# Wider joint projections of two linear attentions, with the gates projected between them

## The chip, the cores and the metric

The kernel runs on one core of a Trainium2 chip. The metric is the device time of one execution in microseconds (us); lower is better.

The engines are named as in the profile: PE multiplies matrices (PEld loads its stationary operand), DVE works on vectors, ACT applies functions and copies, POOL is GpSimd, SP issues most of the transfers. DMA engines move the data.

## The reference

A decoder trunk of two layers over 512 tokens of width 1024. Every layer has a half-step feed-forward block, a mixer and a second feed-forward block. The mixer projects the normalised tokens h once and gives the columns to three groups of heads; the outputs are joined and projected back:

```python
proj = h @ w_in
(g_q, g_k, g_v, g_g, g_lr, n_q, n_kc, n_vc, n_ks, n_vs, n_kw, n_vw, n_gate,
 r_q, r_k, r_v, r_g) = split(proj)
o_gla = rms_norm(gla_chunked(g_q, g_k, g_v, log_a)) * silu(g_g)
o_nsa = nsa_attention(n_q, ...)
o_ret = group_norm(retention_chunked(rotary(r_q), rotary(r_k), r_v)) * silu(r_g)
out = concat([o_gla, o_nsa, o_ret]) @ w_out
```

The first and the third are linear attentions of 4 heads each (256 columns for each of q, k, v and gate). The second is a sparse attention of 8 heads: it adds a compressed, a selected and a windowed softmax attention.

## The kernel before

Every large product is made three times on PE in reduced fp32 form: weights and activations are split into a high part and a low rest (whi, wlo and hh, hl), and high x high, high x low and low x high are summed (mm3, L439 to L445). The weights come as chunks of 128x1024 numbers in an order that plan and plan_mixer write down once (class Weights): a DMA on SP's queue (L164), an ACT copy that makes whi (L176), and a subtraction that makes wlo on DVE, or on POOL for the names in ON_POOL (L177). Chunks are split two ahead of their use; there are three buffers for raw chunks and four for split ones.

The framework has a scheduler of its own: on each engine it may start a later instruction whose inputs are ready while an earlier one waits, and it prefers what is emitted first. So the order in the source is a priority and no fixed sequence. At run time each engine follows the sequence that the scheduler chose.

The mixer of a layer (mixer, L737) emits, in this order:

1. A common unit x (L788 to L790), then the projection vc, with the tokens as the moving operand (proj_t, 24 matmuls of 128x512).
2. The value projection gv of the first linear attention by proj_n (L710): here the tokens are the stationary operand and 256 weight columns move (L721 to L723). It makes 96 matmuls and uses two PSUM banks. Its result is copied to gv by ACT (L817).
3. The compression network of the sparse attention (compress, L901).
4. For each of two head pairs: projections gq and gk, then gla_pair (L932 to L994).
5. Value projection rv (L838), then for each of two pairs: rq, rk with rotary, and ret_pair (L1027 to L1060). rotary (L727) lets ACT make raw (or qraw), SP exchange halves into sw by four DMAs, POOL multiply by the sine (L733) and DVE do the rest (L734, L735).
6. Projections ks, kw and nq0 to nq3 with rotary (krot, qrot, qraw).
7. The temporary pool is closed; the pools of oh, ol, nh, nl and of the sparse attention are opened in its place. nsa (L1084) emits cmp (the compressed softmax, L1123 to L1145), stack_k and stack_q (kh, kl, qk: L1101 to L1113), then gates: proj_n for gg and rg, Silu into sg on ACT (L869), a multiplication by the norm's weights on POOL (L872).
8. lin_out (L1064): the linear outputs onat times their statistics (L1073) and times sg (L1075), transposed on PE (L1078) into oh (ACT, L1080) and ol (DVE, L1081).
9. The weave: score of one unit (query block qc, kind) beside apply of the unit before it. score makes the products (L1162, L1165 to L1167), the maximum on DVE (L1169), the exponentials on ACT (L1172) and the normalisation (L1174 on); apply transposes (L1197), copies (L1200, L1202) and multiplies by the values (L1207). The last apply of a query block ends in nh (L1213).
10. The output projection: the half of the linear attentions, from oh and ol, in the single bank "f" (8 x 12 matmuls, by L443 to L445, and a DVE addition L451), then the half of the sparse attention.

Of eight PSUM banks, three ("mm") and one ("f") rotate through bank(); three "t" serve transposes and small products, and one is "o". The weight chunks of a layer's mixer come in the order x, vc, gv, gq0, gk0, gq1, gk1, rv, rq0, rk0, rq1, rk1, ks, kw, nq0 to nq3, gg, rg, wol, won.

Of the kernel before, what the change touches and what calls it, by code (L numbers as in the profile page):

```python
# [7 lines left out]
F32 = mybir.dt.float32  # L8
# [3 lines left out]
AF = mybir.ActivationFunctionType  # L12
# [12 lines left out]
ON_POOL = ("gg", "gq0", "kw", "rv")  # L25
# [10 lines left out]
def _cols(name, start, n):  # L36
# [11 lines left out]
       for i in range(4)]  # L48
)
N_UNITS = [("gv", _cols("g_v", 0, 256)), ("gg", _cols("g_g", 0, 256)),  # L50
           ("rg", _cols("r_g", 0, 256)), ("rv", _cols("r_v", 0, 256))]
# [161 lines left out]
class Build:  # L213
# [273 lines left out]
    def plan_mixer(self, l):  # L487
        W, a = self.W, self.a

        def n_unit(i):  # L490
            for s in range(2):
                self.u[l, "n", N_UNITS[i][0], s] = W.add(a["wn"][l, i, :, 1024 * s:1024 * s + 1024], D, N_UNITS[i][0] in ON_POOL)

        def t_unit(*names):
            for n in names:
                i = [x[0] for x in T_UNITS].index(n)
                self.u[l, "t", n] = W.add(a["wt"][l, i], D, n in ON_POOL)

        for i in range(KC // 2):
            self.u[l, "x", i] = W.add(a["wx"][l, :, 2 * NXK * i:2 * NXK * (i + 1)], 2 * NXK, i == 2)  # L500
        t_unit("vc")
        n_unit(0)
        t_unit("gq0", "gk0", "gq1", "gk1")
        n_unit(3)
        t_unit("rq0", "rk0", "rq1", "rk1")
        t_unit("ks", "kw", "nq0", "nq1", "nq2", "nq3")
        n_unit(1)
        n_unit(2)
        for key in ("wol", "won"):
            for q in range(KC // 2):  # L510
                self.u[l, key, q] = W.add(a[key][l, q], D)
# [198 lines left out]
    def proj_n(self, l, name):  # L710
        nc = self.nc
        ps = [self.bank((128, 2, 256)) for _ in range(2)]
        for s in range(2):
            wh, wl = self.use(l, "n", name, s)
            for k4 in range(4):
                k = 4 * s + k4
                cs = slice(256 * k4, 256 * k4 + 256)
                for c in range(4):
                    ts = slice(128 * c, 128 * c + 128)
                    o = ps[c // 2][:, c % 2, :]  # L720
                    nc.tensor.matmul(o, self.hh[:, k, ts], wh[:, cs], start=(k == 0 and c % 2 == 0), stop=False)  # L721
                    nc.tensor.matmul(o, self.hh[:, k, ts], wl[:, cs], start=False, stop=False)  # L722
                    nc.tensor.matmul(o, self.hl[:, k, ts], wh[:, cs], start=False,  # L723
                                     stop=(k == KC - 1 and c % 2 == 1))
# [12 lines left out]
    def mixer(self, l):  # L737
# [11 lines left out]
        with tc.tile_pool(name="mtmp", bufs=1, reuse_waits="tile") as tp:  # L749
# [65 lines left out]
            ps = self.proj_n(l, "gv")  # L815
            for i in range(2):
                nc.scalar.activation(gv[:, 2 * i:2 * i + 2, :], ps[i], AF.Copy)  # L817
# [6 lines left out]
            for pr in range(2):  # L824
# [7 lines left out]
                drain(self.gla_pair(l, pr, e, q, k, gv, a2, lrT, onat, stats))  # L832
            self.cos, self.sin = ld("cos", [128, T]), ld("sin", [128, T])
            self.dm, self.gq = ld("dm", [128, 4, 128]), ld("gq", [128, 2, 128])
            rv = tp.tile([128, 4, 256], F32, name="rv", tag="w1", bufs=2)
            ps = self.proj_n(l, "rv")
            for i in range(2):
                nc.scalar.activation(rv[:, 2 * i:2 * i + 2, :], ps[i], AF.Copy)  # L838
# [23 lines left out]
    def gates(self, l, pool):  # L862
        nc, sg = self.nc, self.sg
        ng = pool.tile([128, 2, 64], F32, name="ngb")
        nc.gpsimd.dma_start(ng, self.a["gng"][l:l + 1].to_broadcast([128, 2, 64]))
        for s, n in enumerate(("gg", "rg")):
            ps = self.proj_n(l, n)
            for i in range(2):
                nc.scalar.activation(sg[:, 2 * i:2 * i + 2, s, :], ps[i], AF.Silu)  # L869
            v = sg[:, :, s, :].rearrange("p c (h d) -> p c h d", d=64)  # L870
            for c in range(4):
# [212 lines left out]
    def nsa(self, l, qraw, qrot, krot, vnat, G):  # L1084
# [146 lines left out]
        self.gates(l, np_)  # L1231
# [157 lines left out]
```

## Time and profile before

| | |
|---|---|
| median of 3 executions | 2089.74 us (2088.55 to 2091.99) |
| the profiled execution | 2088.4 us |
| its span in the trace | 2086.6 us |
| PE busy | 2049.2 us, 98% |
| DVE, ACT, POOL busy | 73%, 45%, 31% |

A group of instructions has a busy time, in which overlapping ones count once. Matmuls are pipelined: one that lasts 0.28 us can be followed by the next after 0.12 us, so PE's speed is read from starts, not from durations. The linear-attention stage of layer 0 lies between 400 and 544 us, its sparse attention between 544 and 672; in layer 1 these are 1420 to 1571 and 1571 to 1700.

### The profile page before, as it was taken

How to read it: one execution, taken by the hardware profiler on the slowest of the kernel's cores; microseconds unless marked ns; L12 is line 12 of the kernel's file. 1: busy time of each engine (PE TensorE's matmuls, PEld its weight loads, DVE VectorE, ACT ScalarE, POOL GpSimd, SP SyncE). 2: the span in 40 equal slices, each digit the busy share in tenths (PEclk: the TensorE clock that was granted, in tenths of full speed). 3: DMA queues.
4: the chain of work that ended last, by engine and by line, in shares of the span. 5: the costliest groups of instructions: out<-in, count | busy, mean ns of one | idle time of the engine just before them, and what ended most of it. 6: DMA issues, size and time to landing. Idle time of an engine off the chain costs nothing.

```text
span 2086.6 us, 33098 instructions
## 1 busy us (share of the span) xinstructions
PE 2049.2 (98%) x12954; PEld 1800.2 (86%) x12954; DVE 1516.1 (73%) x2203; ACT 931.3 (45%) x1517; POOL 641.2 (31%) x444
## 2 busy tenths in 40 slices
PE   8999999999999999999999999999999999999998
PEld 6788998987975888899899989989879668989997
DVE  8997894536785799769379749835478759965973
ACT  4432453534575532245354325434527654533543
POOL 1101560312410410046136326413123016623622
PEclk9999999999999999999999999999999999999999
DMA  9697313422310499823322423135232103342312
GB/s 308 228 384 266 102 61 98 153 92 87 107 41 11 155 325 366 311 75 111 114 78 82 123 83 109 55 94 170 78 98 73 41 21 113 102 119 90 106 55 76
DMA packets 93855, 269.43 MB, mean 129 GB/s; under 512 B 10866, under 2 KB 21986, under 8 KB 93699
## 3 DMA queue, kind: packets, MB, share of 16 engines
q1 hardware_dynamic: 92018, 266.06, 38.2%
q8 instruction: 101, 1.65, 0.3%
q0 software_dynamic: 672, 0.58, 0.3%
q10 hardware_dynamic: 1008, 0.69, 0.1%
q14 instruction: 56, 0.45, 0.1%
HBM read 259.94 MB, written 2.10 MB: 126 GB/s over the span
## 4 chain that ended last, share of the span: by engine, by line
PE 90%; DVE 6%; DMA 1%; ACT 1%; issue 1%; POOL 1%; SPq 0%; DVEq 0%; POOLq 0%; ACTq 0%
PE mm L444 24%; PE mm L443 24%; PE mm L445 24%; PE o L1207 2%; PE t L1197 2%; PE mm L722 1%; PE mm L721 1%; PE mm L723 1%; PE mm L1165 1%; DVE wlo L177 1%; DVE adaw L281 1%; PE f L444 1%; PE mm L1166 1%; PE f L443 1%; PE f L445 1%
## 5 line engine op out<-in xcount | busy, mean ns | idle before, releaser
L176 ACT ACTIVATE whi<-wraw 128x1024 fp32r<-128x1024 f32 (+4 forms) x430 | 395.4, 921 | 650.6 <-PE mm L444 558.4
L177 DVE TENSOR_TENSOR wlo<-wraw,whi 128x1024 fp32r<-128x1024 f32 (+3 forms) x410 | 466.0, 1138 | 203.1 <-ACT whi L176 202.2
L443 PE MATMUL mm<-hh,whi 128*128 128x256 f32 (+1 forms) x1736 | 554.1, 323 | 9.6 <-ACT hh L403 9.2
L444 PE MATMUL mm<-hl,whi 128*128 128x256 f32 (+1 forms) x1736 | 559.2, 323 | 4.3 <-DVE hl L374 3.0
L445 PE MATMUL mm<-hh,wlo 128*128 128x256 f32 (+1 forms) x1736 | 557.9, 322 | 0.4 <-DVE wlo L177 0.4
L443 PEld LDWEIGHTS mm<-hh,whi 128*128 128x128 f32 x1736 | 328.9, 191 | 38.1 <-ACT hh L403 11.1
L444 PEld LDWEIGHTS mm<-hl,whi 128*128 128x128 f32 x1736 | 331.8, 191 | 29.4 <-DVE hl L374 3.6
L445 PEld LDWEIGHTS mm<-hh,wlo 128*128 128x128 f32 x1736 | 331.4, 191 | 26.1 <-issue 2.0
L444 PE MATMUL mm<-gl,whi 128*128 128x512 f32 (+1 forms) x792 | 290.2, 366 | 0.0
L445 PE MATMUL mm<-gh,wlo 128*128 128x512 f32 (+1 forms) x792 | 289.5, 366 | 0.0
L443 PE MATMUL mm<-gh,whi 128*128 128x512 f32 (+1 forms) x792 | 287.9, 365 | 0.0
L443 PE MATMUL mm<-t,whi 128*128 128x256 f32 x672 | 190.2, 283 | 0.0
L444 PE MATMUL mm<-t,whi 128*128 128x256 f32 x672 | 190.2, 283 | 0.0
L445 PE MATMUL mm<-t,wlo 128*128 128x256 f32 x672 | 190.2, 283 | 0.0
L281 DVE SCALAR_TENSOR_TENSOR adaw<-adaw,cact 128x1024 f32<-128x1024 f32 x144 | 172.7, 1223 | 0.0
L198 POOL TENSOR_TENSOR wraw<-wraw,sums 128x512 f32<-128x512 f32 x56 | 87.2, 1558 | 271.8 <-DVE wlo L177 271.8
L445 PEld LDWEIGHTS mm<-gh,wlo 128*128 128x128 f32 x792 | 149.4, 189 | 24.0
L444 PEld LDWEIGHTS mm<-gl,whi 128*128 128x128 f32 x792 | 149.4, 189 | 24.0
L443 PEld LDWEIGHTS mm<-gh,whi 128*128 128x128 f32 x792 | 149.3, 189 | 24.0
L451 DVE SCALAR_TENSOR_TENSOR x<-mm,mod,x 128x512 f32<-128x512 f32 (+1 forms) x94 | 62.9, 670 | 144.0 <-PE mm L445 144.0
L190 POOL TENSOR_TENSOR sums<-wraw 128x512 f32<-128x512 f32 x56 | 74.3, 1327 | 280.8 <-PE mm L444 106.5
L326 POOL TENSOR_TENSOR sqa<-sqa,sq 128x512 f32<-128x512 f32 (+1 forms) x44 | 51.3, 1165 | 300.3 <-ACT sq L325 297.8
(325 smaller groups left out, 3621.4 us busy)
## 6 DMA issues: line engine op xcount, KB each, us to landing
wraw<-wfi SPq DMA_DIRECT2D x176, 512.0 KB, 4.1
adaw<-wada SPq DMA_DIRECT2D x144, 512.0 KB, 5.4
wraw<-wfo SPq DMA_DIRECT2D x64, 384.0 KB, 3.1
wraw<-wfo SPq DMA_DIRECT2D x64, 320.0 KB, 3.0
wraw<-wt SPq DMA_DIRECT2D x30, 512.0 KB, 3.4
wraw<-wn SPq DMA_DIRECT2D x16, 512.0 KB, 3.8
w<-w SPq DMA_DIRECT2D x16, 256.0 KB, 4.1
wraw<-wol SPq DMA_DIRECT2D x8, 512.0 KB, 3.7
```

The lines of the kernel that those rows point to most:

```text
L176: self.nc.scalar.activation(h[:, :w], r[:, :w], AF.Copy)
L177: (self.nc.gpsimd if pool else self.nc.vector).tensor_tensor(lo[:, :w], r[:, :w], h[:, :w].bitcast(F32), op=ALU.subtract)
L190: nc.gpsimd.tensor_tensor(s[:, lo], b[:, lo], b[:, hi], op=ALU.add)
L198: nc.gpsimd.tensor_tensor(a[:, hi], a[:, hi], self.sums[:, hi], op=ALU.subtract)
L281: i = nc.vector.scalar_tensor_tensor(w, w, 1.0, self.cact, op0=ALU.mult, op1=ALU.mult, accum_out=self.mod[l][:, f:f + 1])
L326: (nc.gpsimd if d < KC - 2 else nc.gpsimd).tensor_tensor(self.sqa[:, hs], self.sqa[:, hs], sq[:, hs], op=ALU.add)
L443: nc.tensor.matmul(out, wh[:, wk], hh[:, hk], start=start, stop=False)
L444: nc.tensor.matmul(out, wh[:, wk], hl[:, hk], start=False, stop=False)
L445: nc.tensor.matmul(out, wl[:, wk], hh[:, hk], start=False, stop=stop)
L451: nc.vector.scalar_tensor_tensor(xd, p, gate, xd, op0=ALU.mult, op1=ALU.add)
L1197: nc.tensor.transpose(t[:, r, :], p[:, 4 * g + r, 128 * kc:128 * kc + 128], self.ident)
L1207: m = nc.tensor.matmul(o[64 * g:64 * g + 64], vnat[:, kc, c0:c0 + 64], pts[g], start=False, stop=(kind == 1 and kc == qc))
```

## The change

The columns of g_v and r_v become one unit "v" of 512 columns and those of g_g and r_g one unit "g". proj_n makes 96 matmuls of 128x512 for a unit, two token chunks of k at a time, into four banks. v is projected where gv was, and ACT copies its first half to gv and DVE its second half to rv, which now has a tile of its own. The gates are emitted between the two linear attentions, and the order of the weight chunks follows: x, vc, v, gq0, gk0, gq1, gk1, g, rq0, ... nq3, wol, won. Five chunks of a layer's mixer are split on POOL by name, instead of six.

```diff
-ON_POOL = ("gg", "gq0", "kw", "rv")
+ON_POOL = ("gq0", "kw", "v1", "g0", "g2")
...
-N_UNITS = [("gv", _cols("g_v", 0, 256)), ("gg", _cols("g_g", 0, 256)),
-           ("rg", _cols("r_g", 0, 256)), ("rv", _cols("r_v", 0, 256))]
+N_UNITS = [("v", np.concatenate([_cols("g_v", 0, 256), _cols("r_v", 0, 256)])),
+           ("g", np.concatenate([_cols("g_g", 0, 256), _cols("r_g", 0, 256)]))]
...
         n_unit(0)
         t_unit("gq0", "gk0", "gq1", "gk1")
-        n_unit(3)
+        n_unit(1)
         t_unit("rq0", "rk0", "rq1", "rk1")
         t_unit("ks", "kw", "nq0", "nq1", "nq2", "nq3")
-        n_unit(1)
-        n_unit(2)
...
     def proj_n(self, l, name):
         nc = self.nc
-        ps = [self.bank((128, 2, 256)) for _ in range(2)]
-        for s in range(2):
+        ps = [self.bank() for _ in range(4)]
+        for s in range(4):
             wh, wl = self.use(l, "n", name, s)
-            for k4 in range(4):
-                k = 4 * s + k4
-                cs = slice(256 * k4, 256 * k4 + 256)
+            for k2 in range(2):
+                k = 2 * s + k2
+                cs = slice(T * k2, T * k2 + T)
                 for c in range(4):
                     ts = slice(128 * c, 128 * c + 128)
-                    o = ps[c // 2][:, c % 2, :]
-                    nc.tensor.matmul(o, self.hh[:, k, ts], wh[:, cs], start=(k == 0 and c % 2 == 0), stop=False)
...
+                    nc.tensor.matmul(ps[c], self.hh[:, k, ts], wh[:, cs], start=(k == 0), stop=False)
+                    nc.tensor.matmul(ps[c], self.hh[:, k, ts], wl[:, cs], start=False, stop=False)
+                    nc.tensor.matmul(ps[c], self.hl[:, k, ts], wh[:, cs], start=False, stop=(k == KC - 1))
...
             gv = tp.tile([128, 4, 256], F32, name="gv")
-            ps = self.proj_n(l, "gv")
-            for i in range(2):
-                nc.scalar.activation(gv[:, 2 * i:2 * i + 2, :], ps[i], AF.Copy)
+            rv = tp.tile([128, 4, 256], F32, name="rv")
+            ng = tp.tile([128, 2, 64], F32, name="ngb")
+            g2.dma_start(ng, self.a["gng"][l:l + 1].to_broadcast([128, 2, 64]))
+            ps = self.proj_n(l, "v")
+            for c in range(4):
+                nc.scalar.activation(gv[:, c, :], ps[c][:, 0:256], AF.Copy)
+                nc.vector.tensor_copy(rv[:, c, :], ps[c][:, 256:512])
...
                 drain(self.gla_pair(l, pr, e, q, k, gv, a2, lrT, onat, stats))
+            self.gates(l, ng)
             self.cos, self.sin = ld("cos", [128, T]), ld("sin", [128, T])
             self.dm, self.gq = ld("dm", [128, 4, 128]), ld("gq", [128, 2, 128])
-            rv = tp.tile([128, 4, 256], F32, name="rv", tag="w1", bufs=2)
-            ps = self.proj_n(l, "rv")
-            for i in range(2):
-                nc.scalar.activation(rv[:, 2 * i:2 * i + 2, :], ps[i], AF.Copy)
...
+    def gates(self, l, ng):
         nc, sg = self.nc, self.sg
...
+        ps = self.proj_n(l, "g")
+        for c in range(4):
+            nc.scalar.activation(sg[:, c].rearrange("p s n -> p (s n)"), ps[c], AF.Silu)
+        for c in range(4):
+            for s in range(2):
+                v = sg[:, :, s, :].rearrange("p c (h d) -> p c h d", d=64)
                 nc.gpsimd.tensor_tensor(v[:, c], v[:, c], ng[:, s:s + 1, :].to_broadcast([128, 4, 64]), op=ALU.mult)
...
         for qc in range(1, 4):
             stack_q(qc)
-        self.gates(l, np_)
         self.lin_out(l)
```

## Rows read from the trace of the kernel before

**Rows 1.** The page: busy time by engine, and the chain that ended last.

```profile
PE 2049.2 (98%) x12954; PEld 1800.2 (86%) x12954; DVE 1516.1 (73%) x2203; ACT 931.3 (45%) x1517; POOL 641.2 (31%) x444
...
PE 90%; DVE 6%; DMA 1%; ACT 1%; issue 1%; POOL 1%; SPq 0%; DVEq 0%; POOLq 0%; ACTq 0%
```

**Rows 2.** Busy windows by stage, layers 0 and 1: stretch, its us, each engine, clock, DMA.

```profile
400.00:544.24 144.24, 144.24 (x884) 120.07 (x883) 81.99 (x151) 58.73 (x85) 34.28 (x26) 1.00 0.37 116
544.24:579.60 35.36, 35.36 (x284) 33.68 (x283) 27.74 (x37) 25.03 (x47) 15.72 (x15) 1.00 0.35 100
579.60:658.45 78.85, 78.34 (x453) 52.74 (x453) 60.64 (x119) 56.80 (x159) 5.20 (x7) 1.00 0.08 28
658.45:671.84 13.39, 10.43 (x56) 4.48 (x52) 5.46 (x11) 5.24 (x9) 1.27 (x1) 1.00 0.01 1
...
1420.00:1571.40 151.40, 148.42 (x926) 124.48 (x925) 87.74 (x152) 62.45 (x90) 36.59 (x28) 1.00 0.36 110
```

**Rows 3.** PE's timeline around the gates of layer 0: start, us, line, operands.

```profile
544.01 0.40 PE L445 MATMUL mm<-hh,wlo 128*128 128x512 f32 x1
...
571.60 0.28 PE L723 MATMUL mm<-whi,hl 128*128 128x256 f32 x1
571.72 0.60 PE L1078 MATMUL t<-k_k_ident,onat 128*128 128x128 f32 x4
```

**Rows 4.** PE's timeline: matmuls of both widths back to back.

```profile
409.24 0.39 PE L445 MATMUL mm<-hh,wlo 128*128 128x512 f32 x1
409.46 0.39 PE L443 MATMUL mm<-hh,whi 128*128 128x512 f32 x1
...
411.10 0.28 PE L721 MATMUL mm<-whi,hh 128*128 128x256 f32 x1
411.22 0.28 PE L722 MATMUL mm<-wlo,hh 128*128 128x256 f32 x1
```

**Rows 5.** Groups by line and form, PE: one of the three lines of proj_n.

```profile
L721 PE MATMUL mm<-whi,hh 128*128 128x256 f32 x256 | 73.1, 286 | 0.0
```

**Rows 6.** DVE's instructions of L1075 and L177, layer 0: ns min/median/max.

```profile
L1075 DVE TENSOR_TENSOR onat<-onat,sg x4: 675/682/684, 565.7 to 578.0; 128x512 f32<-128x512 f32 x4
...
L177 DVE TENSOR_TENSOR wlo<-wraw,whi x10: 1211/1216/1648, 543.1 to 636.4; 128x1024 fp32r<-128x1024 f32 x10
```

**Rows 7.** Busy windows of 10 us in the weave, layers 0 and 1.

```profile
630.00:640.00 10.00, 10.00 (x53) 5.83 (x51) 8.93 (x17) 7.08 (x16) 0.99 (x1) 1.00 0.13 49
640.00:650.00 10.00, 10.00 (x58) 5.40 (x57) 8.33 (x16) 8.08 (x21) 1.04 (x1) 1.00 0.02 7
...
1660.00:1670.00 10.00, 10.00 (x58) 5.31 (x57) 8.13 (x17) 8.35 (x21) 0.83 (x1) 1.00 0.15 52
1670.00:1680.00 10.00, 9.53 (x55) 5.34 (x53) 8.74 (x17) 7.76 (x21) 1.04 (x1) 1.00 0.00 0
```

**Rows 8.** Windows of PE on "f" tiles alone, by steps of the weave.

```profile
615.86:632.20 16.34, 7.90 (x30) 1.00 0.10 33
...
645.65:658.45 12.80, 0.00 (x0) 1.00 0.00 1
```

**Rows 9.** Timelines of DVE, then ACT, at the start of the sparse attention.

```profile
538.78 4.43 DVE L1073 TENSOR_TENSOR onat<-onat,stats 128x128 f32<-128x128 f32 x16
...
551.07 0.69 DVE L735 TENSOR_TENSOR qrot<-qrot,sw 128x512 f32<-128x512 f32 x1 [1.91 <-POOL sw L733]
551.68 1.28 DVE L1125 TENSOR_TENSOR pc<-t,k_k_cma 128x512 f32<-128x512 f32 x2
...
545.65 0.62 ACT L1102 ACTIVATE kh<-krot 64x512 fp32r<-64x512 f32 x1
```

**Rows 10.** ACT's timeline, layer 0: a table load ahead of the gates' Silu.

```profile
557.86 1.28 ACT L869 ACT_TABLE_LOAD   x1
```

**Rows 11.** Busy windows of 4 us at the norms that follow.

```profile
696.00:700.00 4.00, 2.24 (x15) 2.04 (x16) 4.00 (x7) 2.86 (x8) 3.92 (x3) 0.87 0.37 131
700.00:704.00 4.00, 4.00 (x26) 4.00 (x26) 3.69 (x10) 2.17 (x5) 0.74 (x1) 0.70 0.86 260
```

More of the change, by code (lines that the diff above doesn't have):

```diff
@@ L490, in n_unit @@
         def n_unit(i):
-            for s in range(2):
-                self.u[l, "n", N_UNITS[i][0], s] = W.add(a["wn"][l, i, :, 1024 * s:1024 * s + 1024], D, N_UNITS[i][0] in ON_POOL)
+            for s in range(4):
+                n = N_UNITS[i][0]
+                self.u[l, "n", n, s] = W.add(a["wn"][l, i, :, 1024 * s:1024 * s + 1024], D, f"{n}{s}" in ON_POOL)
         def t_unit(*names):
@@ L711, in proj_n @@
         nc = self.nc
-        ps = [self.bank((128, 2, 256)) for _ in range(2)]
-        for s in range(2):
+        ps = [self.bank() for _ in range(4)]
+        for s in range(4):
             wh, wl = self.use(l, "n", name, s)
-            for k4 in range(4):
-                k = 4 * s + k4
-                cs = slice(256 * k4, 256 * k4 + 256)
+            for k2 in range(2):
+                k = 2 * s + k2
+                cs = slice(T * k2, T * k2 + T)
                 for c in range(4):
                     ts = slice(128 * c, 128 * c + 128)
-                    o = ps[c // 2][:, c % 2, :]
-                    nc.tensor.matmul(o, self.hh[:, k, ts], wh[:, cs], start=(k == 0 and c % 2 == 0), stop=False)
-                    nc.tensor.matmul(o, self.hh[:, k, ts], wl[:, cs], start=False, stop=False)
-                    nc.tensor.matmul(o, self.hl[:, k, ts], wh[:, cs], start=False,
-                                     stop=(k == KC - 1 and c % 2 == 1))
+                    nc.tensor.matmul(ps[c], self.hh[:, k, ts], wh[:, cs], start=(k == 0), stop=False)
+                    nc.tensor.matmul(ps[c], self.hh[:, k, ts], wl[:, cs], start=False, stop=False)
+                    nc.tensor.matmul(ps[c], self.hl[:, k, ts], wh[:, cs], start=False, stop=(k == KC - 1))
         return ps
@@ L860, in mixer @@
         self.nsa(l, qraw, qrot, krot, vnat, G)
-    def gates(self, l, pool):
+    def gates(self, l, ng):
         nc, sg = self.nc, self.sg
[L864 to L871, printed above, removed]
+        ps = self.proj_n(l, "g")
[4 more added lines that the diff above has]
+                v = sg[:, :, s, :].rearrange("p c (h d) -> p c h d", d=64)
                 nc.gpsimd.tensor_tensor(v[:, c], v[:, c], ng[:, s:s + 1, :].to_broadcast([128, 4, 64]), op=ALU.mult)
```

## The prediction

> **What bounds the kernel now.** The page comes first: PE is busy 98% of the span and the chain that ended last is 90% PE [rows 1]. So a change counts by what it does to PE's time: the matmuls it issues, and the stretches in which PE has nothing to do. The windows by stage show what stands beside PE. In the linear-attention stage of layer 0 (400 to 544) PE is never idle and DVE is busy 82 of 144 us; from the last query projection to the end of the sparse attention (544 to 672) PE is full for the first 35.4 us and nearly full for 79 more, but there DVE is busy 27.74 and 60.64 us of it and ACT 25.03 and 56.80; only the last query block's apply leaves PE short [rows 2]. Layer 1 repeats this, with 3 us of PE idle in its linear stage [rows 2]. The second stretch, then, is filled by PE work that does not belong to the attention: the gate projections, then the output projection of the linear half ("f" tiles). PE's own timeline shows the gates: the last matmul of the last query projection (nq3) starts at 544.01, the last gate matmul at 571.60, with the gates' 192 matmuls between, and the transposes of the linear output follow at 571.72 [rows 3].
>
> **The width of the projections.** Back to back, the 128x256 matmuls of L721 to L723 start every 0.120 us, and the 128x512 ones of L443 to L445 every 0.2267 us [rows 4]. There are 256 of each of the three lines, 768 in all [rows 5]; the change makes them 384 of double width. 768 x 0.120 = 92.2 us become 384 x 0.2267 = 87.1: **-5.1 us**, a quarter of it (1.28) for each of the four joint units (two a layer). The rows put the fixed part of one matmul at 2 x 0.120 - 0.2267 = 13 ns. The Trainium skill ("TensorE: Matmul & The Clock Gate", section "Back-to-back issue gap") gives an isolated warm matmul N/2.4 ns and only 2.5 ns fixed; by that the four units would gain 1.0 us, and the whole sum below would be +9.0 instead of +4.9. The trace has the cadence of both widths in long streams, so it decides.
>
> **The cover of the sparse attention's start.** This is the part that costs. Between nq3's last matmul and the first block of weighted scores, ACT and DVE make the compressed softmax, the stacked keys and queries (kh, kl, qk) and the rotary of nq3; PE needs little for that. The 192 gate matmuls, 192 x 0.120 = 23.0 us a layer, fill it. Moved between the linear attentions, they cost their PE time there, where PE is full already (the gain in width is counted above), and the 23.0 us come off here only if the other engines can deliver faster. Count DVE, the busier of the two, up to the last apply: 27.74 + 60.64 = 88.4 us in 114.2 [rows 2]. What leaves: four multiplications of onat by sg, which ran here only because sg came late, 4 x 0.68 = 2.7 [rows 6]; and four of the nine weight splits (wlo), because twelve chunks follow the last query projection now and eight afterwards, 4 x 1.22 = 4.9 [rows 6]. 80.8 us stay. If the stretch shrank by the whole 23.0 us to 91.2, DVE would be busy 89% of it, beside dependent work on ACT and PE. What density does this attention reach? Taken over its stretch 77% [rows 2]. In the three 10-us slices that hold no "f" matmul and both a score and an apply (640 to 650; 1660 to 1680) 83, 81 and 87%, mean 84; the densest slice of layer 0 has 89% [rows 7]. That no filler runs in 640 to 650 the f windows show [rows 8]. I take 84%, because there the attention runs without filler, as it will after the change: 80.8 / 0.84 = 96.2 us, 5.0 more than 91.2. For two layers **+10.0 us**. Ends: at 89% 90.5 us, -0.7 a layer; at 80% (between 84 and the mean of 77) 101.0 us, +9.8 a layer.
>
> A check by the order of the work. In both layers, the first instruction that writes a tile of the next pools follows right behind the last one of the linear stage on its engine: kh behind qraw on ACT (545.65), pc behind qrot on DVE (551.07, then 551.68), kl behind sw on POOL [rows 9]. oh and ol lie in a pool opened at the same point. ol is DVE's, emitted behind cmp and the stacks, and DVE is full without a gap from 551.07 to 559.5 with those. So the output projection, which would have to stand in for the gates, can hardly start before 559, while PE's own work there (scores of the compressed keys, transposes, the first small scores) is little: 35.4 us of the stretch less 23.0 of gates is 12.3, for all of 544 to 579.6 [rows 2]; half of it by 559, an estimate, leaves PE some 9 us a layer without work, of which a part comes back later when PE lags no more. That is of the size of the 5.0.
>
> **Parts costed at nothing.** V's joint unit is evacuated half by ACT and half by DVE, where ACT did all: ACT's part shrinks, DVE gets four copies of 128x256 a layer, no dearer each than its 128x512 product of 0.68 [rows 6], so at most 2.7 us in a stage where DVE has 62 us free; without that cover these would be lost. The five splits on POOL instead of six move one of 1.22 us to DVE in the same stage. The gates' eight POOL multiplications and POOL's load of ngb go to that stage too, where POOL is busy 34 of 144; their cover is the same. The gates' Silu brings one or two table loads of 1.28 us to ACT there and takes two away here [rows 10]; ACT is busy 59 of 144 there, and nothing is late next unless it falls into the decay chain of the second pair, then at most 2.6 us a layer if PE ran dry, which the projections behind prevent. The weights' DMAs are as many and as large; the gates' four chunks are issued on SP ahead of the rotary exchanges (sw); a delay there reaches POOL and DVE, which both have room in that stage, and PE last. Layer 1's 3 us of idle: bound -3 to 0; I take 0, as the late ones are results of DVE that the change doesn't hurry.
>
> **Four banks at once.** The joint units hold all four rotating banks (three mm, one f). The next projection needs the first of them; its last matmul stands nine matmuls, 9 x 0.2267 = 2.0 us, ahead of the unit's end, and its evacuation takes some 0.6, with a table load [rows 10] 1.9. That fits; if the evacuation stands behind a weight copy on ACT, PE waits about 1 us a unit. From 0 to 4 us; I take 0.
>
> **The sum.** -5.1 + 10.0 = **+4.9 us**. The profiled execution took 2088.4 us (its span 2086.6), the median shown is 2089.7, 1.3 above; the sum goes on the median: **2094.6 us**.
>
> **Rivals.** (a) *The output projection fills the gap in time* (the other side). If oh and ol are done when nq3's matmuls end, 8 x 12 x 0.2267 = 21.8 us of "f" matmuls stand where the gates stood, and their absence later costs little, since they delay the attention there: a step of it with 30 of them took 16.34 us, each of the last two, without any, 12.8 with more keys [rows 8]. For it: the multiplications by the statistics are done before 544 already (from 538.78, 4.43 us), and DVE idles 1.91 us before 551 [rows 9]. Against it: the pool order above. Price: the cover costs 0, leaving -5.1, or -8.1 with layer 1's idle: 2084.6 to 2081.6. It decides at the first f matmul: within 5 us of nq3's end this holds, beyond 12 us the forecast. (b) *Half and half*: DVE reaches about 87%, 1.7 us lost a layer, -1.7 in all: 2088.0, no measurable change. (c) *The gap stops the clock*: behind a gap, PE's clock falls to the lower of its levels. In the trace, a stretch of 4 us with PE busy 2.24 was followed by 4 us at a mean granted clock of 0.70, so partly at 1.2 instead of 2.4 GHz [rows 11]. That is some 1.2 us for each such gap; with two gaps a layer and DVE at 80% it is 2104 and more. (d) *The change is none*: a scheduler orders the instructions, so it might keep the gates late. But PE ran the gates ahead of transposes whose inputs were ready some 5 us earlier (onat x sg from 565.7, transposes at 571.72) [rows 3, 6]; what is emitted first goes first. Then only the width would be left, 2084.6; 3%.
>
> **How the numbers follow.** About 0.2% of 2089.7, or 4.2 us, is what a measurement can tell from no change: faster is below 2085.5, slower above 2093.9. Forecast 0.36 and (c) 0.08 make slower 0.44; (a) and (d) 0.30 make faster 0.30; (b) 0.26. The range: low end DVE at 89%, -1.4 - 5.1 = -6.5, 2083; high end DVE at 80%, 19.6 - 5.1 = +14.5, 2104. The forecast's own range is 2091 to 2104.
>
> **What would show it.** Right: 384 matmuls on the projection lines at 0.227 us; PE idle (not above 90% busy) between nq3's end and the first f matmul, some 15 us behind it; DVE at 82 to 88% through the weave, and no f matmul left in its second half. Wrong: f matmuls right behind nq3; the stretch from nq3's last matmul to the last nh under 106 us (127.6 now); or a loss at the joint units, seen as PE waiting for an evacuation behind L721 to L723.

## The result: 1.5% slower, beyond the range

Before 2089.14 us (median of 4 runs beside the changed kernel), after **2119.78 us** (2117.47 to 2124.98); ratio 1.0148, 95% interval [1.0136, 1.0161]. The forecast was 2094.6 with a range of 2083 to 2104. The direction was right, the size was not: +30.6 us where +4.9 was forecast.

### The profile after

The changed kernel's page, for comparison with [rows 1]: TensorE's (PE's) busy time and the clock line of the 40 slices (each about 53 us).

```profile
PE 2060.7 (97%) x12570; PEld 1786.9 (84%) x12570; DVE 1521.5 (72%) x2213; ACT 934.3 (44%) x1519; POOL 635.8 (30%) x442
PEclk9999999999989999999999999999997999999999
```

There are 384 PE matmuls fewer (12954 less 12570), as the joint units make them, yet PE is busy 11.5 us longer, and in two slices the granted clock is down (0.9 or more in all 40 before). The width itself is as forecast: 128 instructions of each of three lines (one of them below), in streams with one start every 0.23 us (482.09, 482.32, 482.55).

```profile
L721 PE MATMUL mm<-whi,hl 128*128 128x512 f32 x128 | 50.1, 394 | 0.0
```

Now the place from which the gates went. PE's timeline of the changed kernel, layer 0, from nq3's last matmul to the first "f" matmul of the output projection (for [rows 3]):

```profile
568.43 0.40 PE L445 MATMUL mm<-hh,wlo 128*128 128x512 f32 x1
...
570.70 2.44 PE L1119 MATMUL t<-kcT,qraw 128*128 128x64 f32 x20
...
594.42 1.94 PE L1139 MATMUL t<-k_k_ident,pc 128*128 128x128 f32 x8 [1.59 <-DVE sm L1171]
596.16 1.73 PE L1074 MATMUL t<-k_k_ident,onat 128*128 128x128 f32 x8
...
598.97 0.47 PE L443 MATMUL f<-oh,whi 128*128 128x512 f32 x1
```

The scores of the compressed keys are done at 573, the softmax over them reaches PE again at 594.4 (the transposes of pc), the linear output's transposes follow, and f starts 30.3 us behind nq3's end (568.66). 15 were forecast. The kernel before has the same transposes of pc here, which the prediction had not looked at:

```profile
569.89 1.03 PE L1143 MATMUL t<-k_k_ident,pc 128*128 128x128 f32 x8
```

That is 25.7 us behind nq3's end (544.24 [rows 2]), against 25.8 in the changed kernel. **The compressed softmax takes as long with the gates as without them.** VectorE's (DVE's) rows of its last step, the mask on pc, say the same; first the kernel before, then the changed one:

```profile
566.91 0.42 DVE L1138 TENSOR_TENSOR pc<-pc,k_k_cmm 128x256 f32<-128x256 f32 x1
```

```profile
593.86 0.41 DVE L1134 TENSOR_TENSOR pc<-pc,k_k_cmm 128x256 f32<-128x256 f32 x1
```

DVE is through with pc 23.1 us behind nq3's end before and 25.6 after; before, the transposes then come another 2.6 us later, among PE's gate matmuls. ScalarE's (ACT's) timeline shows both ends of it, the evacuation of nq3 (qraw) and that of the transposes (pcT); first the kernel before, then the changed one, there with the last nh too:

```profile
545.17 0.58 ACT L729 ACTIVATE qraw<-mm 128x512 f32<-128x512 f32 x1
...
570.52 1.08 ACT L1145 ACTIVATE pcT<-t 128x512 f32<-128x512 f32 x2 [4.13 <-PE t L1143]
```

```profile
569.59 0.58 ACT L726 ACTIVATE qraw<-mm 128x512 f32<-128x512 f32 x1
...
596.40 0.60 ACT L1141 ACTIVATE pcT<-t 128x512 f32<-128x512 f32 x1 [0.25 <-PE t L1139]
...
687.96 0.60 ACT L1209 ACTIVATE nh<-o 128x512 fp32r<-128x512 f32 x1 [2.80 <-PE o L1203]
```

545.17 to 571.60 is 26.4 us, 569.59 to 597.00 is 27.4. In the first, PE had 23.0 us of gate matmuls meanwhile; in the second it had little. The windows of the changed kernel show that, and a smaller loss in the linear stage (columns as in [rows 2]: PE, PEld, DVE, ACT, POOL, then clock and DMA):

```profile
490.00:500.00 10.00, 8.84 (x51) 7.11 (x52) 3.40 (x4) 9.88 (x13) 7.64 (x9) 1.00 0.01 2
500.00:510.00 10.00, 8.78 (x55) 7.00 (x54) 6.65 (x6) 3.21 (x5) 3.79 (x3) 1.00 0.51 144
510.00:520.00 10.00, 8.27 (x34) 5.14 (x35) 6.95 (x19) 1.77 (x3) 1.29 (x2) 0.83 0.21 66
...
570.00:580.00 10.00, 6.66 (x46) 5.08 (x44) 8.85 (x14) 7.20 (x13) 6.94 (x4) 0.85 0.32 92
580.00:590.00 10.00, 7.17 (x23) 4.64 (x22) 9.45 (x16) 7.23 (x28) 0.00 (x0) 0.50 0.00 0
590.00:600.00 10.00, 7.04 (x40) 6.57 (x41) 8.18 (x23) 6.25 (x20) 1.87 (x4) 0.62 0.00 1
...
1620.00:1630.00 10.00, 7.79 (x23) 4.76 (x23) 9.78 (x14) 9.13 (x30) 0.20 (x1) 0.50 0.02 10
```

From 570 to 600 PE is busy 20.9 of 30 us, part of it at the lower of its two clocks (0.50: 1.2 of 2.4 GHz), while DVE is busy 26.5. From pc's first write (577.70) to its last, DVE is all but full, and behind the first f matmul PE is:

```profile
577.70:594.27 16.57, 10.80 (x33) 6.92 (x33) 16.02 (x31) 11.53 (x41) 0.40 (x1) 0.50 0.00 0
...
598.97:688.56 89.59, 86.64 (x488) 54.90 (x486) 62.60 (x113) 58.06 (x146) 5.94 (x6) 1.00 0.08 24
```

Of DVE's 16.0 us the compressed softmax's own steps (L1121 to L1134) are 7.1; the rest are the low parts of keys and queries (L1100, L1109: 4.1) and the first score unit's work (6.1), each counted by its lines, with small overlaps. So what is called the chain below is DVE's sequence in this stretch, with other work between the softmax's steps, and not a row of dependent steps alone. From 490 to 500 it is ACT that is full, 9.88. What it does there (ACT's timeline of the changed kernel, second head pair of the first linear attention, gla_pair):

```profile
486.02 1.28 ACT L933 ACT_TABLE_LOAD   x1
...
487.96 1.28 ACT L864 ACT_TABLE_LOAD   x1
...
490.36 1.28 ACT L942 ACT_TABLE_LOAD   x1
...
492.94 1.28 ACT L864 ACT_TABLE_LOAD   x1
...
494.85 1.28 ACT L945 ACT_TABLE_LOAD   x1
...
496.79 1.28 ACT L864 ACT_TABLE_LOAD   x1
```

L864 is the gates' Silu, L933 the Ln and L942 to L945 the Exp of the decay: Silu and these alternate, and each change loads a table. The kernel before has two loads in this chain (at 475.53 and 478.91), so four are extra; in layer 1 four loads (from 1534.54) stand against two, so two are extra. PE's waits in layer 0 of the changed kernel (line waited for: us in total, times, longest) name both places; S and ke lie behind those Exps, qrot, p and sm in the start of the sparse attention:

```profile
PE mm L1158 <- DVE qrot L732: 3.3, 2, 2.2
PE t L990 <- DVE S L977: 3.0, 1, 3.0
PE mm L1161 <- ACT p L1168: 2.6, 2, 2.0
PE t L1139 <- DVE sm L1171: 1.6, 1, 1.6
PE mm L1158 <- ACT p L1168: 1.6, 1, 1.6
PE t L963 <- POOL ke L947: 1.2, 1, 1.2
```

### Where the time went, in three sums

Five marks of a layer, each a row of a timeline: A, the last vnat evacuation starts; B, nq3's evacuation starts; C, the last pcT evacuation ends; D, the first f matmul starts; E, the last nh ends. In us, layer 0 / layer 1:

| kernel | time | A to B | B to C | D to E | B to E |
|---|---|---|---|---|---|
| before | 2089.1 | 141.6 / 143.2 | 26.4 / 26.4 | 93.9 / 95.2 | 126.7 / 127.7 |
| after | 2119.8 | 166.4 / 167.1 | 27.4 / 26.0 | 89.6 / 89.6 | 119.0 / 118.7 |
| move alone | 2120.7 | 166.0 / 168.7 | 26.8 / 25.7 | 89.6 / 89.6 | 119.2 / 117.2 |
| gates behind retention | 2108.7 | 161.0 / 162.6 | 25.5 / 25.4 | 89.6 / 89.6 | 118.4 / 117.9 |
| gates by Copy | 2111.1 | 161.0 / 163.8 | 27.4 / 26.0 | 89.6 / 89.6 | 120.0 / 118.2 |
| shorter softmax | 2114.1 | 166.2 / 168.7 | 22.8 / 21.8 | 90.4 / 90.4 | 114.6 / 113.6 |
| linear output ahead of ks | 2096.5 | 161.5 / 164.4 | 33.2 / 29.7 | 111.6 / 107.1 | 112.0 / 108.1 |

Layer 0, before to after: the gates' 96 x 0.2267 = 21.8 us come into A to B and the values save 1.3, so +20.5 was due, and +24.8 came: **4.3 lost in the linear stage**. From B to E 23.0 us of gates left, so 103.6 was due, and 119.0 came: **15.3 lost behind nq3**. The width saves 2.6 in all. 4.3 + 15.3 - 2.6 = 17.0; layer 1 in the same way 3.4 + 14.0 - 2.6 = 14.8. Together 31.8, and the spans differ by 2118.4 - 2086.6 = 31.8.

Not all of layer 1's 3.4 us are the table loads. PE's timeline there has a wait that the kernel before has not, ahead of a projection that stands between two parts of the value unit:

```profile
1453.80 0.47 PE L443 MATMUL mm<-hh,whi 128*128 128x512 f32 x1 [2.08 <-DVE k L876]
```

It is for DVE's copies of the compressed keys out of a bank. They stand behind a weight split that took DVE 4.09 us (from 1447.48; 1.22 is usual), while GpSimd split another chunk. From 1454 to 1458 the granted clock is 0.57. All 17 kernels here with the joint value unit have this wait in layer 1, of 1.5 to 2.1 us; the two with narrow units (before, move alone) have none.

### The profile page after: what moved, and what is told of

It reads as the page before. It is cut to its first block, busy times and chain, and to the rows that moved or that the text cites. A ratio compares the mean times of both kernels' runs of the same rounds, so it can differ in the third digit from the quotient of the medians.

```text
span 2118.4 us, 32321 instructions
## 1 busy us (share of the span) xinstructions
PE 2060.7 (97%) x12570; PEld 1786.9 (84%) x12570; DVE 1521.5 (72%) x2213; ACT 934.3 (44%) x1519; POOL 635.8 (30%) x442
## 5 line engine op out<-in xcount | busy, mean ns | idle before, releaser
L177 DVE TENSOR_TENSOR wlo<-wraw,whi 128x1024 fp32r<-128x1024 f32 (+3 forms) x412 | 475.3, 1155 | 235.1 <-ACT whi L176 233.5
L445 PEld LDWEIGHTS mm<-hh,wlo 128*128 128x128 f32 x1736 | 332.0, 191 | 24.8 <-DVE wlo L177 0.6
```

The lines of the kernel that those rows point to most:

```text
L177: (self.nc.gpsimd if pool else self.nc.vector).tensor_tensor(lo[:, :w], r[:, :w], h[:, :w].bitcast(F32), op=ALU.subtract)
L445: nc.tensor.matmul(out, wl[:, wk], hh[:, hk], start=False, stop=stop)
```

## The experiments

### The move or the width

Both joint units kept and the gates put back; only the joint value unit; only the move, with four units of 256 columns.

```diff
         stack...
+        self.gates(l, np_)
         self.lin_out(l)
...
-            self.gates(l, ng)
             self.cos, self.sin = ld("cos", [128, T]), ld("sin", [128, T])
```

> The changed kernel with both joint units of 512 columns, but the gate projections back in their old place ahead of the linear output. Theory (the move costs, the width gains): the width alone gives back 768 matmuls x 0.120 - 384 x 0.2267 = 5.1 us, so 2089.1 - 5.1 = 2084 us (2081 to 2088). Rival (the joint units cost by themselves: four banks held at once, the split evacuation, one VectorE copy more for each chunk): 2090 us or more.

Measured: 2089.28 us, ratio to before 1.0000 [0.9991, 1.0010]. Neither theory's number: the move is the whole loss, but the width gives nothing back either. By the marks, A to E is 1.5 us shorter than before in layer 0 (266.7 for 268.2), where 2.6 were due, and 3.4 longer in layer 1 (274.3 for 270.9). There PE waits 1.6 us for the copies of the compressed keys and 1.1 for onat; no run took these waits away.

> The joint value unit of 512 columns alone: the gates are two units of 256 columns in their old place and order. Theory (the width gains where TensorE is busy; what the joint gates in their old place gave back was their four banks at the start of the sparse attention): 2089.1 - 2.6 = 2086.5 us (2084 to 2088). Rival (the joint value unit itself gives its 2.6 us back, by four banks or by its split evacuation): 2089 us or more.

Measured: 2089.63 us, 1.0003 [0.9994, 1.0012]; the rival's value, though the 2.6 us in question are hardly more than the interval. In layer 0 A to E is 1.2 us shorter, as the 1.3 of a value unit wants; in layer 1 it is 2.9 longer, with 1.5 us of the wait for the copies of the compressed keys (the execution in the trace took 2091.8).

The kernel before with the gates between the linear attentions:

```diff
                 drain(self.gla_pair(l, pr, e, q, k, gv, a2, lrT, onat, stats))
+            self.gates(l, tp)
...
-        self.gates(l, np_)
         self.lin_out(l)
```

> The kernel before with its four units of 256 columns, and only the gates moved between the two linear attentions. Theory (the move costs it all, and the width gives its 5.1 us where TensorE is busy, between the linear attentions): 2119.8 + 5.1 = about 2125 us (2121 to 2128). Rival (the width gives nothing that is not lost again, here too): 2117 to 2121 us. Less than 2115 us would mean that the joint units themselves cost in the changed kernel.

Measured: 2120.67 us, 1.0154 [1.0140, 1.0168], within the rival's range. In layer 0 its marks say why the width is not seen: with the narrow units the Silus come ahead of the second pair's decay and behind it, not between its Exps (table loads at 475.11, 477.06, 479.95 and 483.43, the last for Silu), so the linear stage of layer 0 loses 1.4 us (166.0 - 141.6 - 23.0) and not 4.3. So in layer 0 of the changed kernel the width's 2.6 us are given back as table loads. Layer 1 is not so plain: here too one Silu falls between the Exps (loads at 1526.80, 1528.71 and 1530.65), and 2.5 us are lost; the changed kernel's 3.4 hold the wait at 1453.80. Behind nq3 the loss is 15.6 and 12.6 us, near the changed kernel's 15.3 and 14.0; ACT's timeline of this run, as shown above of the others:

```profile
569.84 0.58 ACT L729 ACTIVATE qraw<-mm 128x512 f32<-128x512 f32 x1
...
596.05 0.60 ACT L1146 ACTIVATE pcT<-t 128x512 f32<-128x512 f32 x1 [0.26 <-PE t L1144]
...
688.45 0.60 ACT L1214 ACTIVATE nh<-o 128x512 fp32r<-128x512 f32 x1 [2.79 <-PE o L1208]
```

### The table loads

The gates to a place without Exp and Ln; and the gates in the changed kernel's place with Copy in place of Silu (the activation left out).

```diff
                 drain(self.ret_pair(l, pr, q, k, rv, onat, stats))
+            self.gates(l, ng)
```

```diff
-            nc.scalar.activation(sg[:, c].rearrange("p s n -> p (s n)"), ps[c], AF.Silu)
+            nc.scalar.activation(sg[:, c].rearrange("p s n -> p (s n)"), ps[c], AF.Copy)
```

> The changed kernel with the gates placed behind the two retention pairs, ahead of ks, where no Exp or Ln runs on ScalarE. Theory (table loads): four of the six loads between 486 and 498 us go, the stretch up to nq3's end gets 3 to 4 us shorter in layer 0 (its end at about 565 us against 568.66) and the time is about 2111 us (2108 to 2114). Rival (the 3.9 us come from elsewhere in the linear stage, such as the two pairs' chains that no gate covers either way): 2116 us or more. Neither theory expects the loss behind nq3 to change by more than 2 us a layer.

> The changed kernel with the gates evacuated by Copy in place of Silu, which leaves the activation out: no Silu stands between the Exp and Ln of the second GLA pair any more, and all else is the same. Theory (table loads): the four extra loads between 486 and 498 us and what they delay are the 3.9 us that the linear stage lost in layer 0, so nq3's end comes at about 564.7 us against 568.66 and the time is 2119.8 - 2 x 5 = about 2110 us (2107 to 2114), as with the gates behind the retention. Rival (the gates' matmuls and banks themselves, wherever their table loads are): 2117 us or more. Neither changes the loss behind nq3.

Measured: 2108.70 us (1.0090 [1.0075, 1.0105]) and 2111.06 us (1.0111 [1.0097, 1.0125]), both in the first theory's range. nq3's evacuation starts at 564.61 and 564.46 in place of 569.59, and the stage is no longer than its matmuls make it: 19.4 us over before in layer 0, 20.5 being due. In the run with the gates behind the retention the second pair has its two loads again, the Silus share one, and PE does not wait (first ACT's timeline, then the windows):

```profile
490.35 1.28 ACT L933 ACT_TABLE_LOAD   x1
...
493.73 1.28 ACT L942 ACT_TABLE_LOAD   x1
...
517.45 1.28 ACT L864 ACT_TABLE_LOAD   x1
```

```profile
490.00:500.00 10.00, 10.00 (x46) 8.27 (x45) 7.65 (x8) 7.82 (x11) 4.21 (x3) 1.00 0.48 140
```

So 9 to 11 of the 31 us go with the alternating Silu and Exp. Some 1.7 of them (an estimate, 4 x 0.43) are layer 1's 4 us at a clock of 0.57; in these two runs the clock there is 1.00, though the wait ahead of it is the same. The Trainium skill ("ScalarE: Activation LUTs", section "Table sets: the hidden batching unit") asks for activations to be batched by table set; this case agrees, with 1.28 us for each load and a linear stage (A to B) that is 3.3 to 5.4 us a layer shorter without the alternation.

### Bank, order, or a chain behind nq3

First theory: the linear output's transposes, whose inputs are ready between 570 and 577, wait for one of three "t" banks. Two edits: the output stage emitted ahead of the compressed softmax; and its transposes in "mm" banks.

```diff
+        self.lin_out(l)
         cmp()
         stack_k()
...
-        self.lin_out(l)
```

```diff
-                t = self.pt([128, 4, 128])
+                t = self.pt([128, 4, 128], "mm")
```

> The changed kernel with one line moved: the output stage of the linear attentions is emitted ahead of the compressed softmax. Theory (bank order): in the changed kernel the linear output's transposes wait, with their inputs ready 20 us before, for a t bank that the compressed softmax's transposes hold, so the output projection starts 30 us behind nq3's end; given their banks first, the first f matmul comes within 15 us of nq3's end, the stretch from nq3's last matmul to the last nh falls from 119.3 to about 108 us in layer 0, the granted clock of that stretch stays above 0.9, and the time is 2118.4 - 2 x 11 = about 2096 us (2088 to 2104). Rival (VectorE's density, as forecast): VectorE has the same work in the same stretch and sets its end, the stretch stays within 4 us of 119.3 and the time is 2111 us or more.

> The changed kernel with the linear output's four transposes put into mm banks in place of t banks, nothing moved. Theory (bank order): the t banks alone held them back, so the first f matmul comes within 15 us of nq3's end and the time falls by 10 to 25 us, to 2093 to 2108 us; it may fall less than with the output stage emitted first, since the scores want the mm banks. Rival (VectorE's density): as before, 2111 us or more. If emitting the stage first gains and this does not, it was the order of the instructions on VectorE and TensorE, not the bank.

Measured: 2117.05 us (1.0127 [1.0107, 1.0146]) and 2127.97 us (1.0179 [1.0150, 1.0208]). f came early, at 582.8 and 581.1, as the theory wanted, and the time did not follow: **the theory fell.** The compressed softmax came late instead (pcT ends at 613.7 and 601.8), and the apply of each query block starts from it (o<-pcT,vb). The windows of the first, where PE is full but at the lower clock:

```profile
570.00:580.00 10.00, 4.45 (x33) 3.28 (x32) 6.98 (x16) 1.94 (x3) 7.65 (x4) 0.88 0.44 131
580.00:590.00 10.00, 10.00 (x35) 7.71 (x35) 5.88 (x9) 9.79 (x16) 0.00 (x0) 0.50 0.00 0
590.00:600.00 10.00, 10.00 (x39) 8.54 (x38) 7.17 (x11) 6.21 (x34) 0.00 (x0) 0.50 0.00 0
```

Second theory: the clock. Matmuls that nobody reads fill PE's idle time: 64 a layer in the changed kernel, 70 where the linear output is first, then 25 in the changed kernel (the edit shown).

```diff
+        def keep(n, src):
+            for _ in range(n):
+                nc.tensor.matmul(dum, self.ident, src, start=True, stop=True)
...
+                keep(5, qraw[:, 3, 0:128])
...
+                if (qc, kind, h0) in ((0, 0, 0), (0, 0, 4), (0, 1, 0)):
+                    keep(5, qrot[:, 3, 0:128])
```

> The changed kernel with 64 matmuls of 128 columns that nobody reads, 24 behind the two halves of the compressed scores and 40 behind the first two score units, so that TensorE is not idle while it waits for VectorE; no other work is moved. Theory (clock): the granted clock of 580 to 600 us stays at 1.00 against 0.50 and 0.62, the scores and transposes there run at full speed, and the time falls by 3 to 8 us a layer, to about 2108 us (2103 to 2114). Rival (VectorE and ScalarE set the pace of the gap whatever TensorE's clock): the clock is 1.00 and the time still 2117 us or more.

> The run with the linear output emitted first, with 70 matmuls of 128 columns that nobody reads in TensorE's two idle stretches behind nq3 (570 to 580 us); else the same. Theory (clock): there the clock fell to 0.50 for 578 to 601 us while TensorE was busy all the time, 20 busy us at half speed, so with the clock kept the same work takes 10 us less a layer: 2117 - 2 x 9 = about 2099 us (2093 to 2106). Rival (VectorE sets the pace): 2114 us or more at a clock of 1.00.

> The changed kernel with 25 matmuls of 128 columns a layer that nobody reads (64 in the earlier run), five behind each half of the compressed scores and five behind each of the first three score units: some 5.8 us by the earlier run's 0.235 us for each, less than the 9 us that TensorE idles there. Theory (half clock has a price of its own): the granted clock stays at 0.9 or more behind nq3 and the time falls by half of the 18.9 us lost to the half clock or more, to 2110 us or less (2102 to 2111). Rival (the scores and transposes at half clock only take the place of waiting for VectorE): 2116 us or more with the clock at 1.00. A clock that falls all the same leaves it open.

Measured: 2120.18, 2122.13 and 2120.92 us (1.0149 [1.0134, 1.0165], 1.0160 [1.0146, 1.0174], 1.0154 [1.0139, 1.0168]); no gain in any. In the first two the clock is 1.00 in all of 570 to 600, but their fillers take 15 us a layer and more, above the idle time, so alone they decide little. (In the first, pcT does come 2.5 and 1.5 us closer to nq3, and B to E is 1.6 and 1.3 us shorter, 117.4 and 117.3; its time is no lower.) The run with 25 is the cleaner one. Its windows:

```profile
570.00:580.00 10.00, 8.67 (x72) 7.94 (x72) 8.83 (x12) 7.20 (x12) 6.05 (x4) 1.00 0.30 80
580.00:590.00 10.00, 6.29 (x39) 4.86 (x37) 9.75 (x20) 7.70 (x35) 0.40 (x1) 0.80 0.00 1
590.00:600.00 10.00, 8.33 (x47) 7.67 (x48) 8.13 (x18) 5.64 (x13) 1.47 (x3) 0.69 0.01 2
...
1620.00:1630.00 10.00, 7.93 (x55) 6.38 (x53) 9.75 (x14) 8.89 (x32) 0.00 (x0) 1.00 0.01 2
```

Layer 1 keeps 1.00 to 1630, where the changed kernel had 0.50; PE waits 2.1 of those 10 us all the same, DVE is at 9.75 as it was at 9.78, and the end does not move. Matmuls at half clock only took the place of waiting. The clock did not stay up throughout, so a small price of its own, 1 or 2 us a layer, is not excluded; the 9 us and more that the theory wanted are.

Third theory: the time from nq3 to pcT is a chain over DVE and ACT with its own length, whatever PE does. Two runs shorten it: the low parts of keys and queries to GpSimd; and, left out of the computation, the normalisation and gates of the compressed softmax.

```diff
-                nc.vector.tensor_tensor(qk[og, g], qrot[gs, :, qs], qk[gs, g].bitcast(F32), op=ALU.subtract)
+                nc.gpsimd.tensor_tensor(qk[og, g], qrot[gs, :, qs], qk[gs, g].bitcast(F32), op=ALU.subtract)
```

```diff
-            nc.vector.tensor_reduce(m8, pc, axis=AX.X, op=ALU.add)
-            nc.vector.reciprocal(m8, m8)
...
-            nc.vector.tensor_tensor(m4, m4, gk, op=ALU.mult)
-            nc.vector.tensor_tensor(pc, pc, mb, op=ALU.mult)
```

> The changed kernel with the low parts of the stacked keys and queries (ten subtractions of 64x512 a layer, 0.67 to 0.71 us each, seven of them between nq3 and the linear output's transposes) made by GpSimd in place of VectorE; GpSimd stands idle from 580 to 590 us. Theory (VectorE's chain sets the gap): VectorE has 4.2 us less between the compressed scores and their transposes, so those come 3 to 4 us earlier and the time falls by 4 to 8 us, to about 2113 us (2110 to 2116). Rival (the gap is a chain of latencies over several engines, not VectorE's time): within 2 us of 2119.8 us. GpSimd's own slower operation may hold the scores of the second block up and make it slower than both.

> The changed kernel without the normalisation and the gates of the compressed softmax (its sum, reciprocal and two multiplications on VectorE, 1.22 + 0.34 + 0.20 + 1.22 = 3.0 us by the changed kernel's timeline, with the waits between them); the rest is as it was. Theory (the chain behind nq3 sets when the output projection can begin, and that the end): pcT and the first f matmul come 3 to 5 us earlier in each layer, the 89.6 us behind the first f matmul stay, and the time falls by 6 to 10 us to about 2112 us (2109 to 2115). Rival (it is the amount of work behind nq3, not this chain): f comes earlier and the end does not, 2117 us or more.

Measured: 2117.87 us (1.0140 [1.0125, 1.0155]) and **2114.13 us (1.0110 [1.0092, 1.0128])**. The first is at the edge of the rival's range and inconclusive: pcT is 2.6 us closer to nq3 in layer 0, as it should, but GpSimd needs 1563 ns for what took DVE 686, and the interval overlaps the changed kernel's. The groups of L1109, first of this run, then of the changed kernel:

```profile
L1109 POOL TENSOR_TENSOR qk<-qrot,qk 64x512 fp32r<-64x512 f32 x12 | 18.8, 1563 | 9.6 <-ACT qk L1108 8.8
```

```profile
L1109 DVE TENSOR_TENSOR qk<-qrot,qk 64x512 fp32r<-64x512 f32 x12 | 8.2, 686 | 0.4
```

The second is in the theory's range. ACT's and PE's timelines of it:

```profile
569.37 0.58 ACT L726 ACTIVATE qraw<-mm 128x512 f32<-128x512 f32 x1
...
591.05 1.08 ACT L1135 ACTIVATE pcT<-t 128x512 f32<-128x512 f32 x2
...
683.41 0.60 ACT L1203 ACTIVATE nh<-o 128x512 fp32r<-128x512 f32 x1 [2.80 <-PE o L1197]
```

```profile
593.66 0.48 PE L443 MATMUL f<-oh,whi 128*128 128x512 f32 x1
```

3.0 us of DVE work out of the chain bring pcT 4.6 us closer to nq3 in layer 0 (22.8 for 27.4), f 5.3 us and the last nh 4.6 us earlier than in the changed kernel, with 90.4 us from f to the end. So in the changed kernel's order the chain sets when f can begin, and the end follows f. Its length is DVE's work and the order of it rather than the waits between the steps: from pc's first write to its last DVE is busy 16.02 of 16.57 us in the changed kernel, 10.06 of 10.61 here, and 12.00 of 13.99 with the low parts on GpSimd. Nor is the length fixed: with the output stage first it was 42.7 us, and with the gates back in their old place 35.4. No run put the softmax's steps ahead of the first scores' on DVE.

### Another cover

If PE only lacks work behind nq3, the output projection can be that work, if its inputs are early: the linear output stage ahead of ks (temporaries closed first, for room), with the gates behind the retention or between the two.

```diff
+            tp_cm.__exit__(None, None, None)
...
+            self.lin_out(l)
             for i, n in enumerate(("ks", "kw")):
...
-        self.lin_out(l)
```

> Both joint units, the gates behind the retention pairs, and the linear output stage ahead of ks in place of inside the sparse attention, so that the output projection's 96 matmuls are ready when nq3 ends (the pool of temporaries is closed before it, which makes room for its tiles). Theory (cover: TensorE lacks work in the gap because only the output projection could fill it and it comes 25 to 30 us late): no extra table loads, the first f matmul within 3 us of nq3's end, no stretch of 10 us behind nq3 below 9.5 busy us, and a time of about 2086 us (2078 to 2096). Rival (VectorE's work sets the end of the sparse attention whatever TensorE has): f runs early and the second half of the attention starves in its place, 2102 us or more.

> The changed kernel with the gates between the linear attentions as it has them, and the linear output stage ahead of ks as in the run before. Theory (cover plus table loads): the gap behind nq3 is filled, the linear stage still loses its 4 to 6 us a layer, so about 10 us above the run with the gates behind the retention: 2096 us (2090 to 2106). Rival (VectorE sets the end): 2112 us or more.

Measured: 2096.47 us (1.0046 [1.0033, 1.0058]) and 2120.41 us (1.0156 [1.0140, 1.0171]). The first is just above its theory's range. It gains 12.2 us over the same place of the gates without it: f begins at 565.8, 1.4 us behind nq3's end, and B to E falls from 118.4 and 117.9 to 112.0 and 108.1. Of the 14.8 and 13.2 us lost behind nq3 with that place of the gates, 6.4 and 9.8 come back. Its pcT is late (ends at 598.6, 33.2 us behind nq3), which may hold the rest; no run shows it. The second gains nothing, the rival's value: f begins at 572.7, but pcT ends only at 611.2. Why f in that place delays the softmax by 8 us more was not settled. Three combinations were run to take off what was left: the low parts on GpSimd on top of this, and on top of the gates in their old place; and gates and linear output emitted ahead of the compressed softmax in the old place.

> Gates behind the retention, linear output ahead of ks (2096.5 us), and the low parts of stacked keys and queries on GpSimd. Theory (VectorE's load behind nq3 sets what is left): VectorE was at 9.76 and 9.81 of 10 us from 580 to 600 and loses 4 to 7 us of work there, so the time falls by 4 to 10 us to about 2090 us (2086 to 2093). Rival (latency chain, or GpSimd's slowness): 2094 us or more.

> Both joint units, the gates in their old place, and the low parts of stacked keys and queries on GpSimd. Theory (VectorE's load): what the joint gates in the old place lost again, 2 to 5 us, comes back, 2084 us (2081 to 2087), below the kernel before. Rival (VectorE does not set it): 2088 us or more.

> Both joint units, the gates in their old place, but gates and linear output emitted ahead of the compressed softmax and the stacking. Theory (order against the compressed softmax): the output projection starts earlier and covers the rest of the start, 2083 us (2079 to 2087). Rival (the compressed softmax is then late, as in the run with the linear output first, where its transposes came at 612.6 us): 2090 us or more.

Measured: 2095.51 (1.0029 [1.0020, 1.0038]), 2096.22 (1.0032 [1.0020, 1.0044]) and 2092.37 us (1.0017 [1.0009, 1.0026]): the rival each time. On GpSimd the low parts cost 6.9 us where the gates already cover the chain (2096.2 against 2089.3). No version beat the kernel before.

## Why the prediction was wrong in size

- **The width** (-5.1): the cadence was right, 0.227 us. In the linear stage it shows with the gates behind the retention, which add 19.4 us there where narrow units would need 23.0 for the gates alone. In layer 0 of the changed kernel the joint gates' table loads take it back; in layer 1 the value unit's wait at 1453.80 takes a part of it in every run with that unit.
- **"nothing is late next unless it falls into the decay chain of the second pair, then at most 2.6 us a layer if PE ran dry, which the projections behind prevent."** This step failed. It does fall there, with four extra loads in layer 0 and two in layer 1, and PE ran dry: 4.3 us in layer 0, and in layer 1 a part of 3.4. The chain was named and then covered by a sentence without a row: what PE had left to do behind that pair was not counted.
- **"80.8 / 0.84 = 96.2 us, 5.0 more than 91.2."** This step failed, and it is the large one: 15.3 and 14.0 us a layer in place of 5.0. It divided DVE's work over the whole stretch by a density taken from its middle, as if one engine set the pace of one stream. There are two parts with different limits: up to the transposes of pc DVE is busy 24.0 of 25.8 us, and f has not begun; behind f's start PE is busy 86.6 of 89.6 us. The first part, the chain, did not shrink at all (26.4 before, 27.4 after); of the 23.0 us of gates that left, only 7.7 came off, in the weave and just ahead of it: D to E 4.3, C to D 4.4, less the chain's 1.0. DVE's density in the weave is no limit either: after the change its windows from 620 to 680 hold 14.2 to 15.7 of 20 us, not the 82 to 88% forecast. The 80.8 was too small as well: up to the last apply DVE was busy 84.6 us (568.66 to 675.17, 13.4 us ahead of the last nh's end as in [rows 2]). Four weight splits left, as forecast, but the four multiplications of onat by sg stayed in layer 0 (569.63 to 577.18).
- **The check by the order of the work** saw the mechanism (the output projection "can hardly start before 559", pc behind qrot on DVE) but stopped at its first half: the rest of the softmax, from pc's first write to its transposes, is 16.7 us more (577.70 to 594.42) and was not counted. The row that shows it, 569.89 above, stands among the last gates, just ahead of [rows 3]'s 571.72.
- **Rival (c)**, the clock, at 0.08: the clock did fall, and 2104 "and more" holds the result, but by the runs with fillers the clock is an effect of the gap and at most a small part of its price. Rival (a) asked for f within 5 us of nq3's end; three runs made that true in layer 0 (f 1.4, 3.8 and 1.4 us behind it) and still took 2096.5, 2120.4 and 2095.5, so (a)'s "the cover costs 0" was wrong too. Rival (d) is out: the gates did move.
- **V's split evacuation and four banks at nothing:** no wait for an evacuation of the joint units stands among layer 0's waits. In layer 1 the nothing was wrong: the wait of 2.1 us at 1453.80, and the clock of 0.57 behind it. That it comes with the joint value unit the 17 kernels against two show; whether the four banks, the split on GpSimd or the order on DVE makes it, no run separates.

## What to carry to other kernels

Before moving independent matmuls away from a place, read when the dependent chain beside them starts and ends: if it ends as the matmuls do, they are hiding it, and it will stand there bare. An engine's density averaged over a stretch hides where it is full and others wait for it: here DVE is at 93% for 26 us and at 71 to 79% behind them. And give a moved activation a place where its table is already loaded: two functions of different tables that alternate on one chain cost a load at each change.

## What the runs showed of the hardware

In the run with the linear output first, PE was busy 4.45 of 10 us, and the granted clock was then 0.50 for the 20 us from 580 to 600 with PE busy in all of them. A 64x512 subtraction took GpSimd 1563 ns and DVE 686. A weight split of 128x1024, 1.22 us on DVE as a rule, took it 4.09 us from 1447.48 in the changed kernel, while GpSimd made one too (from 1448.08, 2.41 us). None of these was in the rows of before.
